# Queries and keys kept as two float16 halves, all score passes on 128 rows, recurrence mixes stored tile by tile

## The chip, the cores and the metric

The kernel runs on one core of one Trainium2 chip. The metric is the time in microseconds (us) that the device takes for one execution. Matrix products run on TensorE (PE; its weight loads are shown as PEld), elementwise work and reductions on VectorE (DVE), activations and casts on ScalarE (ACT), further elementwise work on GpSimd (POOL). SyncE (SP) issues nearly all DMA transfers, one behind another.

## What is computed

One layer of a trunk with two groups of heads that read the same normalised input, 128 context tokens and 1024 latent tokens (T = 1152 columns), model width 1024. Cut to what bears on the change:

```python
p = h @ w_in                                     # h: modulated rms norm of x
q, k, v, g_att, x_lru, g_lru = jnp.split(p, SPLITS, axis=-1)
q, k = axial_rope(q), axial_rope(k)              # latent tokens only
k_all = concatenate([ctx_k, k], axis=1)          # 128 cached keys, of the latent queries' own cache
s = einsum('bqhmd,bkhmd->bhmqk', qblk, k_all) / sqrt(64)   # 8 heads, 2 maps m of 64 wide keys each
p = softmax(s); a = p[:, :, 0] - lam * p[:, :, 1]
o = einsum('bhqk,bkhe->bqhe', a, v_all)
att = rms_norm(o, g_subln) * (1 - lam_init) * silu(g_att)
lru = (hf + hb) * silu(g_lru)                    # scans in both directions over gated inputs
x_new = x + gate * rms_norm(concatenate([att, lru]) @ w_out, g_post)
```

The outputs are the new tokens, the keys and values of the context tokens, and the final states of the scans.

## The kernel before

Every engine works through its instructions in the order in which the program writes them, and so does SP with its DMAs: the order is written out by hand, and a wait holds all that stands behind it on its engine. Tiles come from pools with a fixed number of buffers per tag, and a new tile waits for the last reader of the buffer that it takes.

Float32 matrix operands are kept as a rounded part and a remainder (hi and lo), and a product is three passes, hi by hi, hi by lo and lo by hi (`mm3`, L117 to L119). The projection is computed in blocks of 128 outputs, each of three chunks of 384 columns, each chunk 24 matmuls (`chunk`).

The first stretch of the program works through the eight blocks of the recurrence: two projections and two gates per block on PE, the scans on DVE. `mix_send` writes each block's result to scratch in DRAM, in groups of four blocks (`mixg`). Then come the queries, keys and values (`qk_block`, `v_block`). In a block of queries or keys, `qk_chunk` copies each chunk out of PSUM on ACT; `tick()` after each chunk runs closures that `after(d, fn)` put d ticks later. When the three chunks are there, `rope` rotates the latent columns on DVE (L770 to L773), one tick later `halves` splits the block into hi (a cast on ACT, L745) and lo (a subtraction on POOL, or on DVE for the first block), and one tick after that `send` stores them to the scratch `qs[h]` or `ks`. In the scratch a query tile holds three things for each of 128 queries: the hi part of either map, each written twice (rows 0 to 63 and 64 to 127), and one slot with the lo part of both. For each map the scratch of the keys holds hi in one half of the rows, lo in the other. The cached keys of all heads are loaded, split and stored once (`cached_keys`). Between the blocks stand sums for the gate vector of the output (L930), which wait for a DMA. The first q blocks share the engines with the end of the recurrence's last block (L581 is the square root of its coefficients).

The second stretch is attention, 72 periods of 8 heads by 9 query tiles of 128. Per period PE computes two score maps (`scores`), the product with the values four periods back (`pv`, float16 halves of 128 columns), and pieces of the projection by w_out (`po`). One score map is six passes over 384 keys at most:

```python
PE.matmul(sps[:, j, :w_], lhsT=qt[:, mp], rhs=kt_[:, mp, c], ...)          # L1076: q hi twice x [k hi; k lo]
PE.matmul(sps[:, j, :w_], lhsT=qt[rows, 2], rhs=kt_[rows, mp, c], ...)     # L1078: q lo x k hi, 64 rows
```

DVE takes the maximum out of PSUM (L1085), for the first map adds a small constant (L1088), and ACT computes the exponential out of the same PSUM tile with the row sum (L1092); two such PSUM tiles exist. `recip` and `combine` then form the factor of the second map (L1100, L1102), the difference of the maps (L1111), and its two float16 halves (ACT L1114, POOL L1115), which a DMA transposes for `pv`. Last come the remaining parts of the projection and the output's norm.

Of the kernel before, what the change touches and what calls it, by code (L numbers as in the profile page):

```python
# [10 lines left out]
F32 = mybir.dt.float32  # L11
# [12 lines left out]
NH = 8  # L24
# [74 lines left out]
def hybrid_step_kernel(ctx: ExitStack, tc: tile.TileContext, io):  # L99
# [21 lines left out]
    qs = [dr.tile([P, 3, T], F32R, name=f"qs{h}") for h in range(NH)]  # L121
    ks = dr.tile([P, 2, NH, T + CTX], F32R, name="ks")
    vs = [dr.tile([P, 2, 2, 10, P], F16, name=f"vs{i}") for i in range(NH // 2)]
    sgs = [dr.tile([P, T], F32, name=f"sgs{h}") for h in range(NH)]
    mixg = [dr.tile([P, len(g), 2, T], F32R, name=f"mix{i}") for i, g in enumerate(GROUPS)]
    mix = {kt: mixg[i][:, j] for i, g in enumerate(GROUPS) for j, kt in enumerate(g)}
# [19 lines left out]
    lsig = const.tile([P, 1], F32, name="lsig")  # L146
    gsub = const.tile([P, 1], F32, name="gsub")
# [55 lines left out]
    def load_k(h, mp):  # L203
        if mp == 0:
            kts[h] = kp.tile([P, 2, T + CTX], F32R, tag="kt", name=f"kt{h}")
        move(out=kts[h][:, mp], in_=ks[:, mp, h])
# [5 lines left out]
    def load_q(n):  # L212
        h, i = tiles[n]
        qts[h, i] = kp.tile([P, 3, P], F32R, tag="qt", name=f"qt{h}_{i}", bufs=5)
        move(out=qts[h, i], in_=qs[h][:, :, i * P:(i + 1) * P])

    with ExitStack() as pa:
# [409 lines left out]
        def mix_send(n):  # L627
            for i, m in enumerate(blk.pop(n)["mix"]):
                move(out=mix[KT + n][:, i], in_=m)
# [5 lines left out]
        def next_chunk(n, j):  # L635
# [7 lines left out]
            else:  # L643
                if j == 0:
                    blk["q0"] = lp.tile([P, T], F32, tag="u", name="qfq0")
# [96 lines left out]
        def split_store(t_, w_, name, tags=("a", "w")):  # L742
            hi = lp.tile([P, T], F32R, tag=tags[0], name=f"hi{name}")
            lo = lp.tile([P, T], F32R, tag=tags[1], name=f"lo{name}")
            S.copy(out=hi[:, :w_], in_=t_)  # L745
            split_lo(V if name in ('q0',) else G, lo[:, :w_], t_, hi[:, :w_])
            return hi[:, :w_], lo[:, :w_]

        def cached_keys():
            ck = lp.tile([P, NH * P], F32, tag="xp", name="ck")  # L750
            nc.sync.dma_start(out=ck, in_=io["cache_kT"].rearrange("p h c -> p (h c)"))
            cks = []
            after(2, lambda: cks.extend(split_store(ck, NH * P, "ck")))

            def send():
                for mp in range(2):
                    for part in range(2):
                        r = 64 * (mp ^ part)
# [797 lines left out]
```

## Time and profile before

| | |
|---|---|
| median of 3 runs | 1295.27 us (1294.48 to 1301.24) |
| profiled execution: own time, span | 1297.48 us, 1295.1 us |
| PE, PEld busy | 1220.8 us (94% of the span), 1069.4 us (83%) |
| DVE busy | 968.3 us (75%) |
| ACT, POOL busy | 680.1 us (53%), 479.1 us (37%) |
| mean granted clock of PE | 0.978 of full speed |

The span reaches from the first to the last instruction of the profiled execution; its own time, 2.4 us longer, is what the device counted for the same execution. Busy shares are means over stages with different limits. Matmuls are pipelined, so the duration that the profile gives for one covers a part of the next; what a row of matmuls takes is read from one start to another.

### The profile page before, as it was taken

To read this page: it belongs to the slowest core of one execution; us is meant where nothing else is said; L and a number is where in the kernel's file an instruction comes from. 1 tells how busy PE (TensorE), PEld (TensorE's weight loads), DVE (VectorE), ACT (ScalarE), POOL (GpSimd) and SP (SyncE) were. 2 spreads that over 40 slices of the span, in tenths; PEclk is the share of its full clock that TensorE was granted. 3 is DMA by queue.
4 is the path that set the end of the run, shared out by engine and by line. 5 is a ranking of instruction groups with operands and counts; after the bars stand their busy time and mean duration, and the time that the engine had idled before them with its cause. 6 is when DMAs were issued, how large, how long until landed. Compare 5 with 4: busy or idle time off the path is not lost.

```text
span 1295.1 us, 19733 instructions
## 1 busy us (share of the span) xinstructions
PE 1220.8 (94%) x7672; PEld 1069.4 (83%) x7672; DVE 968.3 (75%) x1253; ACT 680.1 (53%) x1152; POOL 479.1 (37%) x244
## 2 busy tenths in 40 slices
PE   6899999999999899999999699999999989999887
PEld 1499999999999899989999577776777766777666
DVE  4938779777979828666473257888898989899977
ACT  4446545654665233332232357677667676766632
POOL 0421112111212334424242214346655566555624
PEclk9999999999999899999999899999999998999999
DMA  9221222123212757446272659899899988899864
GB/s 364 103 72 41 91 93 93 60 74 111 76 54 102 214 165 220 151 161 167 88 218 68 228 127 201 193 214 249 174 214 224 226 218 191 201 207 217 205 202 167
DMA packets 262916, 208.62 MB, mean 161 GB/s; under 512 B 158876, under 2 KB 228252, under 8 KB 262056
## 3 DMA queue, kind: packets, MB, share of 16 engines
q1 hardware_dynamic: 262536, 206.52, 59.0%
q8 instruction: 60, 0.98, 0.3%
q10 hardware_dynamic: 288, 0.85, 0.2%
q14 instruction: 32, 0.26, 0.1%
HBM read 112.16 MB, written 56.90 MB: 131 GB/s over the span
## 4 chain that ended last, share of the span: by engine, by line
PE 67%; DVE 20%; issue 4%; DMA 4%; ACT 3%; SPq 1%; POOL 1%; DVEq 0%; ACTq 0%; POOLq 0%
PE s L1078 5%; DVE mx L1085 4%; PE s L1076 4%; PE po L117 3%; DVE e L1111 3%; PE ga L119 3%; PE ga L117 3%; PE ga L118 3%; PE po L119 3%; PE po L118 3%; PE v L118 2%; PE v L117 2%; PE v L119 2%; PE x L118 2%; PE x L119 2%
## 5 line engine op out<-in xcount | busy, mean ns | idle before, releaser
L114 POOL TENSOR_TENSOR wlo<-wraw,whi 128x1024 fp32r<-128x1024 f32 x48 | 129.5, 2698 | 421.6 <-ACT whi L262 418.0
L1115 POOL TENSOR_TENSOR a<-e,a 128x1152 f16<-128x1152 f32 (+1 forms) x72 | 156.0, 2166 | 212.3 <-ACT a L1114 210.3
L1085 DVE TENSOR_REDUCE mx<-s 128x1 f32<-128x1152 f32 (+1 forms) x144 | 176.8, 1233 | 65.8 <-PE s L1078 64.1
L1092 ACT ACTIVATE e<-s,mx 128x1152 f32<-128x1152 f32 (+1 forms) x144 | 162.4, 1128 | 77.0 <-DVE fa L1100 29.7
L1111 DVE SCALAR_TENSOR_TENSOR e<-e,fa,e 128x1152 f32<-128x1152 f32 (+1 forms) x72 | 119.0, 1653 | 6.7 <-DVE fa L1102 0.5
L1076 PE MATMUL s<-kt,qt 128*128 128x384 f32 (+1 forms) x400 | 100.3, 355 | 19.5 <-ACT e L1092 18.0
L117 PE MATMUL po<-woh,lt 128*128 128x512 f32 x216 | 97.2, 450 | 16.3 <-ACT e L1092 13.9
L1114 ACT CAST a<-e 128x1152 f16<-128x1152 f32 (+1 forms) x72 | 76.0, 1055 | 60.8 <-DVE e L1111 52.7
L1078 PE MATMUL s<-kt,qt 64*128 64x384 f32 (+1 forms) x400 | 107.0, 369 | 0.0
L117 PE MATMUL pv<-vt,t 128*128 128x128 f16 x584 | 103.5, 222 | 1.9 <-ACT ot L1130 1.9
L118 PE MATMUL pv<-vt,t 128*128 128x128 f16 x584 | 102.8, 220 | 0.0
L119 PE MATMUL pv<-vt,t 128*128 128x128 f16 x584 | 102.8, 220 | 0.0
L1076 PEld LDWEIGHTS s<-kt,qt 128*128 128x128 f32 x400 | 69.1, 192 | 31.8 <-ACT e L1092 24.3
L1078 PEld LDWEIGHTS s<-kt,qt 64*128 64x128 f32 x400 | 63.7, 187 | 34.8 <-issue 34.2
L119 PE MATMUL po<-woh,lt 128*128 128x512 f32 x216 | 86.7, 401 | 0.0
L118 PE MATMUL po<-wol,lt 128*128 128x512 f32 x216 | 86.6, 401 | 0.0
L117 PE MATMUL v<-whi,hTh 128*128 128x256 f32 x288 | 81.8, 284 | 0.0
L119 PE MATMUL v<-whi,hTl 128*128 128x256 f32 x288 | 81.5, 283 | 0.0
L118 PE MATMUL v<-wlo,hTh 128*128 128x256 f32 x288 | 81.5, 283 | 0.0
L117 PEld LDWEIGHTS po<-woh,lt 128*128 128x128 f32 x216 | 41.4, 192 | 41.1 <-issue 15.9
L117 PEld LDWEIGHTS <-t 128*128 128x128 f16 x584 | 57.5, 98 | 17.7 <-issue 17.5
L117 PE MATMUL k<-hTh,whi 128*128 128x384 f32 x192 | 66.4, 346 | 4.8 <-ACT qfk L633 4.8
(299 smaller groups left out, 3588.0 us busy)
## 6 DMA issues: line engine op xcount, KB each, us to landing
wraw<-in_w_in_dram SPq DMA_DIRECT2D x48, 512.0 KB, 3.5
qt<-qs SPq DMA_DIRECT2D x72, 192.0 KB, 3.6
lt<-mix SPq DMA_DIRECT2D x27, 512.0 KB, 4.6
kt<-ks SPq DMA_DIRECT2D x16, 640.0 KB, 6.2
qs<-hiq SPq DMA_DIRECT2D x32, 288.0 KB, 5.8
wa<-in_w_ada_dram SPq DMA_DIRECT2D x16, 512.0 KB, 10.9
wor<-in_w_out_dram SPq DMA_DIRECT2D x32, 256.0 KB, 3.3
mix<-amo SPq DMA_DIRECT2D x6, 1152.0 KB
```

Source lines behind the costliest of these rows:

```text
L114: eng.tensor_tensor(out=lo, in0=val, in1=f(hi), op=ALU.subtract)
L117: PE.matmul(out, lhsT=lh, rhs=rh, start=start, stop=False)
L118: PE.matmul(out, lhsT=lh, rhs=rl, start=False, stop=False)
L119: PE.matmul(out, lhsT=ll, rhs=rh, start=False, stop=stop)
L1076: PE.matmul(sps[:, j, :w_], lhsT=qt[:, mp], rhs=kt_[:, mp, c], start=True, stop=False)
L1078: PE.matmul(sps[:, j, :w_], lhsT=qt[rows, 2], rhs=kt_[rows, mp, c], start=False, stop=True)
L1085: V.tensor_reduce(out=d["mx"][:, mp:mp + 1], in_=sv, axis=AX.XY, op=ALU.max, negate=True)
L1092: S.activation(out=e_[:, :nk].rearrange("p (j c) -> p j c", c=w_), in_=sv, func=AF.Exp, bias=d["mx"][:, mp:mp + 1], accum_out=total)
L1111: V.scalar_tensor_tensor(out=e1, in0=e1, scalar=d["fa"], in1=e0, op0=ALU.mult, op1=ALU.subtract)
L1114: S.copy(out=a16[:, 0:nk], in_=e1)
L1115: G.tensor_tensor(out=a16[:, nk:2 * nk], in0=e1, in1=a16[:, 0:nk], op=ALU.subtract)
```

## The change

Queries and keys are now kept as float16 halves. Each head's q and k block gets a unit, a power of two: ACT squares the block and sums along the rows (`squares`), PE sums that over the partitions with a matrix of ones (`un`, one column), and four small operations on DVE make the power of two from the bits of the sum (`power`; for keys two more keep the factor `back` that undoes both units). ACT scales into the hi half, DVE forms the lo half in one operation. Loading, storing and reading follow that:

- q has four slots per tile: hi and lo of either map, each written twice. The scratch lies tile by tile, so that a tile is one piece of 1 KB per row; the store is eight DMAs in pieces of 256 bytes. A q tile shrinks from 192 to 128 KB, the keys of a head from 640 to 320 KB.
- The cached keys of a head are loaded into the block's own tile, behind its 1152 columns, and handled with it; `cached_keys` is gone.
- Both sets of score passes take 128 rows. The maximum of each map is multiplied by `back` (one more small operation for the second map), the exponential takes it as its scale. The factor of the second map is made by a tensor_scalar.
- The recurrence's mixes of the first two groups are stored tile by tile, in pieces of 512 bytes, and read back in pieces of 4 KB. The mixes of the attention get two buffers of one tag; the gate vector lies in two tiles.

```diff
+            def squares():
+                d["sq"] = lp.tile([P, 1], F32, tag="qsq", name=f"sq{name}")
+                junk = lp.tile([P, T + CTX], F32, tag="gs0" if early else "a", name=f"j{name}")
+                S.activation(out=junk[:, :w_], in_=t_[:, :w_], func=AF.Square, accum_out=d["sq"])
...
-            def halves(tags=("a", "w")):
-                d["hl"] = split_store(t_, T, name, tags)
+            def power():
+                tp = small(f"un{name}")
+                PE.matmul(tp[:, 0:1], lhsT=onesf, rhs=d["sq"], start=True, stop=True)
+                V.tensor_scalar(out=unit, in0=tp[:, 0:1], scalar1=2.0 ** -60, scalar2=None, op0=ALU.max)
+                ui = unit.bitcast(I32)
+                V.tensor_scalar(out=ui, in0=ui, scalar1=0x7FFFFFFF, scalar2=1, op0=ALU.bitwise_and,
+                                op1=ALU.logical_shift_right)
+                V.tensor_scalar(out=ui, in0=ui, scalar1=-1, scalar2=0x663759DF, op0=ALU.mult, op1=ALU.add)
+                V.tensor_scalar(out=ui, in0=ui, scalar1=0x7F800000, scalar2=None, op0=ALU.bitwise_and)
+                if which:
+                    V.tensor_tensor(out=back[:, h:h + 1], in0=unit, in1=qksc[:, 0, h:h + 1], op=ALU.mult)
+                    V.reciprocal(out=back[:, h:h + 1], in_=back[:, h:h + 1])
+
+            def halves():
+                power()
+                d["hl"] = lp.tile([P, 2, T + CTX], F16, tag="gs2" if early else "w", name=f"hl{name}")
+                hi, lo = (d["hl"][:, x, :w_] for x in range(2))
+                S.activation(out=hi, in_=t_[:, :w_], func=AF.Copy, scale=unit)
+                V.scalar_tensor_tensor(out=lo, in0=t_[:, :w_], scalar=unit, in1=hi, op0=ALU.mult, op1=ALU.subtract)
...
+                        if which:
                             r = 64 * (mp ^ part)
-                            move(out=ks[r:r + 64, mp, h, 0:T], in_=val[64 * mp:64 * mp + 64])
+                            nc.sync.dma_start(out=ks[r:r + 64, h, mp], in_=half)
+                        else:
+                            for r in (slice(0, 64), slice(64, 128)):
+                                nc.sync.dma_start(out=qs[h][r, :, 2 * part + mp],
+                                                  in_=half[:, :T].rearrange("p (t c) -> p t c", t=NT))
...
+            squares()
             if which:
                 after(1, context_keys)
+            rope(t_, name)
+            after(1, halves)
+            after(2, send)
...
-                PE.matmul(sps[:, j, :w_], lhsT=qt[rows, 2], rhs=kt_[rows, mp, c], start=False, stop=True)
+                PE.matmul(sps[:, j, :w_], lhsT=qt[:, 2 + mp], rhs=kt_[:, mp, c], start=False, stop=True)
...
             if mp == 0:
-                V.tensor_scalar(out=d["mx"][:, 0:1], in0=d["mx"][:, 0:1], scalar1=lsig, scalar2=None, op0=ALU.add)
+                V.tensor_scalar(out=d["mx"][:, 0:1], in0=d["mx"][:, 0:1], scalar1=unit, scalar2=lsig, op0=ALU.mult,
+                                op1=ALU.add)
+            else:
+                V.tensor_scalar(out=d["mx"][:, 1:2], in0=d["mx"][:, 1:2], scalar1=unit, scalar2=None, op0=ALU.mult)
...
-            V.scalar_tensor_tensor(out=d["fa"], in0=d["fa"], scalar=lam, in1=kqs[h][:, i:i + 1], op0=ALU.mult,
-                                   op1=ALU.mult)
+            V.tensor_scalar(out=d["fa"], in0=d["fa"], scalar1=lam, scalar2=kqs[h][:, i:i + 1], op0=ALU.mult, op1=ALU.mult)
```

The order of instructions shows three places. The first is ACT where the recurrence ends and the queries begin: `w7_1` is the root of the last coefficients, `q1_1` and `q1_2` are the second and third chunk of head 1's queries, `k0_0` the first of head 0's keys, `hiq0` the hi part of head 0's queries, `whi13` a weight's. Before:

```order
L581 ACTIVATE w7_1_3197<-w7_1_3197 128x1158 [waits DVE_49]
L633 ACTIVATE qfq1_3163<-q1_1_3207 128x384 [waits PE_49]
L745 CAST hiq0_3242<-qfq0_3022 128x1152 [waits DVE_49]
L633 ACTIVATE qfq1_3163<-q1_2_3246 128x384 [waits PE_49]
L262 CAST whi13_3315<-wraw26_3052 128x1024 [waits DMAHW5_49,Pool_49]
L633 ACTIVATE qfk0_3289<-k0_0_3290 128x384 [waits DVE_49,PE_49]
```

Of the change (`jq0` and `jq1` are the squares, `hlq0` the hi half):

```order
L585 ACTIVATE w7_1_3199<-w7_1_3199 128x1158 [waits DVE_49]
L768 ACTIVATE jq0_3205,sqq0_3204<-qfq0_3024 128x1152
L637 ACTIVATE qfq1_3165<-q1_1_3212 128x384 [waits PE_49]
L794 ACTIVATE hlq0_3253<-qfq0_3024,qksc_102 128x1152 [waits DVE_49]
L637 ACTIVATE qfq1_3165<-q1_2_3256 128x384 [waits PE_49]
L768 ACTIVATE jq1_3298,sqq1_3297<-qfq1_3165 128x1152 [waits Activation_49]
L266 CAST whi13_3332<-wraw26_3054 128x1024 [waits DMAHW5_49,Pool_49]
L637 ACTIVATE qfk0_3305<-k0_0_3307 128x384 [waits DVE_49,PE_49]
```

Two passes over a whole block, the squares of q0 and of q1, now stand between the copies out of PSUM; the hi half waits for DVE's unit.

The second place is PE just behind the first chunk of head 0's keys, in the change:

```order
L118 MATMUL k0_0_3307<-hTl7_138,whi12_3050 128x384
L119 MATMUL k0_0_3307<-hTh7_130,wlo12_3051 128x384
L779 MATMUL unq1_3341<-sqq1_3297,onesf_91 128x1 [waits Activation_49]
L117 MATMUL k0_1_3350<-hTh0_123,whi12_3050 128x384
L118 MATMUL k0_1_3350<-hTl0_131,whi12_3050 128x384
```

Before, the matmuls of `k0_1` followed those of `k0_0`; now the one-column matmul `unq1` stands between, and waits for ACT's squares. There is one such matmul in each of the 16 blocks of queries and keys; `unq0` stands behind chunk `q1_1`.

The third is DVE in a period of the attention, query tile 40 and 41 (`s` is a score map in PSUM, `mx` its negated maximum, `kq` the sum of the first map, `sm` that of the second). Before:

```order
L1085 TENSOR_REDUCE mx41_9354<-s41_0_9356 128x1 [waits PE_49]
L1088 TENSOR_SCALAR mx41_9354<-mx41_9354,lsig_101 128x1 [waits DVE_49]
L1100 RECIPROCAL fa40_9404<-sm40_9282 128x1 [waits Activation_49]
L1102 SCALAR_TENSOR_TENSOR fa40_9404<-fa40_9404,lam_100,kq4_8973 128x1 [waits DVE_49]
L1111 SCALAR_TENSOR_TENSOR e40_1_9327<-e40_1_9327,fa40_9404,e40_0_9293 128x1152 [waits DVE_49,Pool_49]
L1085 TENSOR_REDUCE mx41_9354<-s41_1_9413 128x1 [waits PE_49]
L1085 TENSOR_REDUCE mx42_9434<-s42_0_9436 128x1 [waits PE_49]
```

Of the change:

```order
L1093 TENSOR_REDUCE mx41_9563<-s41_0_9565 128x1 [waits PE_49]
L1096 TENSOR_SCALAR mx41_9563<-mx41_9563,back_103,lsig_101 128x1 [waits DVE_49]
L1111 RECIPROCAL fa40_9613<-sm40_9490 128x1 [waits Activation_49]
L1113 TENSOR_SCALAR fa40_9613<-fa40_9613,lam_100,kq4_9177 128x1 [waits DVE_49]
L1121 SCALAR_TENSOR_TENSOR e40_1_9536<-e40_1_9536,fa40_9613,e40_0_9501 128x1152 [waits DVE_49,Pool_49]
L1093 TENSOR_REDUCE mx41_9563<-s41_1_9622 128x1 [waits PE_49]
L1099 TENSOR_SCALAR mx41_9563<-mx41_9563,back_103 128x1 [waits DVE_49]
L1093 TENSOR_REDUCE mx42_9644<-s42_0_9646 128x1 [waits PE_49]
```

One operation of 128x1 comes in behind the second map's maximum, and the factor is made by another kind of operation; the order is otherwise that of before.

## Rows read from the trace of the kernel before

**Rows 1.** Windows view, three stages: busy per engine, clock, DMA share, GB/s.

```profile
106.00:395.00 289.00, 286.86 (x1650) 286.54 (x1648) 240.60 (x207) 165.18 (x187) 50.63 (x20) 1.00 0.23 79
480.00:720.00 240.00, 237.71 (x1557) 234.98 (x1556) 144.23 (x203) 75.49 (x143) 81.68 (x29) 0.99 0.49 147
840.00:1224.00 384.00, 362.39 (x2589) 276.56 (x2587) 342.33 (x458) 265.12 (x519) 225.46 (x122) 0.98 0.93 212
```

**Rows 2.** The page's chain that ended last, shares of the span by line.

```profile
PE s L1078 5%; DVE mx L1085 4%; PE s L1076 4%; PE po L117 3%; DVE e L1111 3%; PE ga L119 3%; PE ga L117 3%; PE ga L118 3%; PE po L119 3%; PE po L118 3%; PE v L118 2%; PE v L117 2%; PE v L119 2%; PE x L118 2%; PE x L119 2%
```

**Rows 3.** Groups of instructions by line, the attention stage.

```profile
L1078 PE MATMUL s<-kt,qt 64*128 64x384 f32 (+1 forms) x400 | 107.0, 369 | 0.0
...
L1076 PE MATMUL s<-kt,qt 128*128 128x384 f32 (+1 forms) x400 | 100.3, 355 | 19.5 <-ACT e L1092 18.0 <-DMA qt<-qs 1.1
...
L1111 DVE SCALAR_TENSOR_TENSOR e<-e,fa,e 128x1152 f32<-128x1152 f32 (+1 forms) x72 | 119.0, 1653 | 6.7 <-DVE fa L1102 0.5
...
L1102 DVE SCALAR_TENSOR_TENSOR fa<-fa,lam,kq 128x1 f32<-128x1 f32 x72 | 45.2, 628 | 2.1
...
L1088 DVE TENSOR_SCALAR mx<-mx,lsig 128x1 f32<-128x1 f32 x72 | 15.3, 212 | 2.1
```

**Rows 4.** Timeline of PE and its weight loads: value passes, one score call.

```profile
803.07 0.23 PE L117 MATMUL pv<-vt,t 128*128 128x128 f16 x1
...
804.53 0.22 PE L119 MATMUL pv<-vt,t 128*128 128x128 f16 x1
...
996.16 0.77 PE L1076 MATMUL s<-kt,qt 128*128 128x384 f32 x3
...
996.86 0.47 PEld L1078 LDWEIGHTS s<-kt,qt 64*128 64x128 f32 x3 [0.25 <-issue]
...
997.58 0.50 PE L117 MATMUL po<-woh,lt 128*128 128x512 f32 x1
```

**Rows 5.** Waits from 754 to 1224 us, DVE: total us, times, longest.

```profile
DVE mx L1085 <- PE s L1078: 45.0, 46, 2.9
```

**Rows 6.** Timeline of DVE and POOL around one lambda factor.

```profile
938.36 1.26 POOL L1040 TENSOR_TENSOR acc<-acc,ev 128x512 f32<-128x512 f32 x1
...
938.73 0.91 DVE L1102 SCALAR_TENSOR_TENSOR fa<-fa,lam,kq 128x1 f32<-128x1 f32 x1
...
939.74 1.42 DVE L1111 SCALAR_TENSOR_TENSOR e<-e,fa,e 128x1152 f32<-128x1152 f32 x1
```

**Rows 7.** Timeline of ACT, DVE and PE from the recurrence into the queries.

```profile
409.24 2.24 ACT L581 ACTIVATE w<-w 128x1158 f32<-128x1158 f32 x2
...
411.16 0.33 PE L117 MATMUL k<-hTh,whi 128*128 128x384 f32 x1
...
414.24 1.16 ACT L745 CAST hiq<-qfq 128x1152 fp32r<-128x1152 f32 x1 [2.39 <-DVE qfq L773]
...
415.30 0.48 ACT L633 ACTIVATE qfq<-q 128x384 f32<-128x384 f32 x1
...
425.61 1.35 DVE L114 TENSOR_TENSOR loq<-qfq,hiq 128x1152 fp32r<-128x1152 f32 x1
...
437.06 0.69 PE L117 MATMUL k<-hTh,whi 128*128 128x384 f32 x1 [4.82 <-ACT qfk L633]
```

**Rows 8.** Timeline of SP, DVE and ACT around the first gate-row sum.

```profile
583.17 3.33 SPq L110 DMA_DIRECT2D qs<-hiq  x4
...
592.83 0.68 DVE L930 TENSOR_TENSOR gb<-gacc,gb 2x512 f32<-2x512 f32 x1 [9.22 <-DMA gb<-in_b_gate_dram]
...
594.22 1.29 DVE L770 STREAM_SHUFFLE rsk<-qfk 128x1024 f32<-128x1024 f32 x1
...
597.94 1.23 DVE L773 TENSOR_TENSOR qfk<-qfk,rsk 128x1024 f32<-128x1024 f32 x1
...
605.33 0.43 ACT L836 COPY vf<-v 128x128 f32<-128x128 f32 x2 [2.38 <-PE v L119]
```

**Rows 9.** Groups of instructions by line: TensorE's one-column float32 matmul.

```profile
L417 PE MATMUL ssq<-onesf,qsum 128*128 128x1 f32 x18 | 2.2, 251 | 0.0
```

More of the change, by code (lines that the diff above doesn't have):

```diff
@@ L644, in next_chunk @@
                 if j == 0:
[L645 removed]
+                    blk["q0"] = lp.tile([P, T + CTX], F32, tag="u", name="qfq0")
                 qk_chunk(0, 0, blk["q0"], j)
@@ L740, in hybrid_step_kernel @@
         swap = [(i + 16) % 32 for i in range(32)]
[L742 to L758, printed above, removed]
-                        move(out=ks[r:r + 64, mp, :, T:],
-                             in_=cks[part][64 * mp:64 * mp + 64].rearrange("p (h c) -> p h c", h=NH))
-            after(2 + 1, send)
-        after(9, cached_keys)
         after(24, weight)
         def rope(t_, name):
-            lat = t_[:, CTX:]
+            lat = t_[:, CTX:T]
             rs = lp.tile([P, LAT], F32, tag="xp", name=f"rs{name}")
@@ L776, in qk_block @@
             name = f"{'qk'[which]}{h}"
-            if (which, h) == (0, 0):
-                t_ = blk["q0"]
-                after(1, lambda: rope(t_, name))
-                after(2, lambda: halves(("gs0", "gs2")))
-                after(3, lambda: send())
-            else:
-                t_ = lp.tile([P, T], F32, tag="u", name=f"qf{name}")
-                for j in range(NCH):
-                    qk_chunk(which, h, t_, j)
-                    tick()
-                rope(t_, name)
-                after(1, lambda: halves(("gs0", "gs2") if (which, h) == (0, 1) else ("a", "w")))
-                after(2, lambda: send())
+            w_ = T + CTX if which else T
+            first, early = (which, h) == (0, 0), (which, h) < (0, 2)
+            t_ = blk["q0"] if first else lp.tile([P, T + CTX], F32, tag="u", name=f"qf{name}")
+            unit = qksc[:, which, h:h + 1]
+            d = {}
+            def squares():
+                d["sq"] = lp.tile([P, 1], F32, tag="qsq", name=f"sq{name}")
+                junk = lp.tile([P, T + CTX], F32, tag="gs0" if early else "a", name=f"j{name}")
+                S.activation(out=junk[:, :w_], in_=t_[:, :w_], func=AF.Square, accum_out=d["sq"])
             def context_keys():
@@ L809, in send @@
+            def halves():
[4 more added lines that the diff above has]
+                V.scalar_tensor_tensor(out=lo, in0=t_[:, :w_], scalar=unit, in1=hi, op0=ALU.mult, op1=ALU.subtract)
+            def send():
+                for part in range(2):
                     for mp in range(2):
-                        for part, val in enumerate((hi, lo)):
+                        half = d["hl"][64 * mp:64 * mp + 64, part]
+                        if which:
@@ L815, in qk_block @@
+            if which:
+                nc.sync.dma_start(out=t_[:, T:], in_=io["cache_kT"][:, h])
+            if first:
+                after(1, lambda: (squares(), rope(t_, name)))
+                after(2, halves)
+                after(3, send)
+                return
+            for j in range(NCH):
+                qk_chunk(which, h, t_, j)
+                tick()
+            squares()
             if which:
                 after(1, context_keys)
+            rope(t_, name)
+            after(1, halves)
```

54 lines of the change are left out of this document (24 added, 30 removed).

## The prediction

> **What bounds the kernel now.** I read the stretches first, then the chain that ended last, then line groups and waits of attention, and last the timeline where the change adds waits. In the stretches [rows 1] the reader is to see that PE is busy nearly all the time in each, that DVE has much room among the queries and keys (144.2 of 240 us) and little in attention (342.3 of 384), and that the granted clock there is 0.98, all but full. The chain [rows 2] gives 5% and 4% of the span to the two sets of score passes, 117 us, and another 7% to DVE's maximum and its difference of the maps: attention is bound by PE with DVE close behind. Its DVE waits 45.0 us in all for score passes, in 46 waits [rows 5]; that is all that it could give if PE were no limit.
>
> **Score passes.** A call of six full passes takes 1.42 us from its first start to the next product's start (996.16 to 997.58), 0.237 per pass [rows 4]. The same 384 columns take 289/1650 = 0.175 us in the recurrence's projections, where all passes have 128 rows [rows 1]. So the excess lies with the 64-row set: its weight loads begin only at 996.86, after 0.25 us of idle time in the loading queue, one for each change between 128 and 64 rows. What float16 does is seen at the values: 26 steps of 128 columns from 803.07 to 804.53 are 0.056 each, 0.168 for 384 [rows 4]. A call becomes 6 x 0.168 = 1.01, at the other bound 6 x 0.175 = 1.05; I take 0.41 off. Two maps of 64 latent tiles make 128 full calls, 128 x 0.41 = 53 us of PE. Of 128 x 1.42 = 182 us the chain held 117, 64%, so **-34**. Bounds: if it counts only where DVE stood waiting, 46 x 0.41 = -19; at most -45 [rows 5]. The Trainium skill ("TensorE: Matmul & The Clock Gate", Part 3: packing small matmuls) says that a weight load overlaps a running matmul only when it addresses other rows of the array, which speaks against 128-row passes. The trace disagrees: full-row passes, each with a load of its own, keep the pace above [rows 1, 4]. By the page's rule nothing would be gained here.
>
> **Small operations.** The unit of the second map's maximum is one more tensor_scalar per period; that of before takes 212 ns [rows 3], so 72 x 0.212 = 15.3 us. It stands ahead of the exponential that frees the PSUM tile. I take half, **+8** (0 if DVE's waits swallow it, +15 if none do). The factor's operation averages 628 ns, three times that, 45.2 us in all [rows 3]; in one instance it runs 938.73 to 939.64 and ends with POOL's operation of 938.36 + 1.26 = 939.62 [rows 6]. A tensor_scalar is nearer to 0.212, and 45.2 - 15.3 = 30 us come free. But if it is the third operand that has DVE wait for POOL, the difference of the maps behind it has one too; its mean of 1653 ns against 1.42 alone [rows 3, 6] shows that it already waits. So only **-5** (0 to -30). The wait would be late in the next operation instead.
>
> **The units' matmuls.** 16 columns of ones at 0.25 us [rows 9]: **+4**, without their waits.
>
> **First place: the recurrence into the queries.** ACT ends the roots at 411.48 [rows 7]. The squares of q0 (1.16, as the hi cast of the same tile) end at 412.6. PE's `unq0` stands behind chunk q1_1; the next chunk q1_2 took 24 x 0.173 = 4.2 and ended at 411.16, so PE is at `unq0` at 407.0 and waits 5.6. Then q1_2 and k0_0 run to 421.0, and PE meets `unq1`. That needs the squares of q1, which on ACT stand behind a copy (0.48) and the hi half of q0, which waits for DVE's unit; DVE comes to that place at 425.61, where the lo part of q0 is now. 425.61 + 4 x 0.212 + 1.16 + 0.48 + 1.16 = 429.3, so PE waits 8.3. What goes is the wait of 4.82 at 437.06, whose cause (ACT behind the same place) is overtaken. 5.6 + 8.3 - 4.8 = **+9** (+5 if the copies come early, +14 if the old wait stays).
>
> **Second place: the gate vector.** DVE's sum waits 9.22 us for its DMA, to 592.83 [rows 8]. That DMA stands on SP behind a q store whose issues take 3.33/4 = 0.83. There are three more, +2.5, and they start later by power and hi, 0.85 + 1.16 = 2.0. The sum moves to 597.3; behind it on DVE stands the rope of the next keys. From 597.3: 1.39 to the rope, 4.95 for it, 6 x 0.212 for the unit, 1.16 for hi, two copies of 0.48 and 1.16 for squares give 608.2, where ACT copies out the values for which PE had come at 605.33 [rows 8]. That is 2.9, and 1 to 3 more for the units' matmul behind the same DVE queue: **+6** (0 if the DMA's own landing decides, +14 if the whole 4.5 counts at the sums behind too).
>
> **What I cost at nothing.** In the blocks of queries and keys DVE gets the unit (0.85 to 1.27), the lo half (1.42, as the difference of the maps) and the wait for hi (1.16), 3.4 to 3.9 us. A block is 72 x 0.175 = 12.6 us of PE; DVE now uses 144.2/240 of it, 7.6, and 11.0 to 11.5 stay under. The cover ends when DVE needs 1.1 to 1.6 us more per block. POOL is relieved of its subtraction (its share is 81.7 of 240). ACT trades a cast for a scaling and adds squares (1.16 per block) at 75.5 of 240 [rows 1]. The smaller loads of q and keys and the longer pieces of the mixes give nothing that PE waits for: score passes wait 1.1 us in all for q [rows 3]. The tail's tiles and gate rows change only buffers: nothing. If DMA room matters, it is where the share is 0.93, in attention [rows 1], and there it falls.
>
> **Sum.** -34 + 8 - 5 + 4 + 9 + 6 = **-12** on the profiled execution's own 1297.5 us (2.4 over its span), so 1285.5. That execution is 2.2 above the median of 1295.27; against the runs this is 1283 to 1284, and I say **1284**.
>
> **Rivals.** Half a per cent, 6.5 us, is about what a measurement here can tell from no change.
> 1. *The gain runs deeper*: all 45 us of DVE's waits go, the small operation hides, the gate place costs nothing: -45 + 0 - 5 + 4 + 5 = -41, 1254. For it: PE is on 64% of the calls. Against: DVE is busy 89% of attention and gets more. 0.13.
> 2. *PE's clock falls*: more idle time on PE would bring stretches at the lower of its two levels (1.2 and 2.4 GHz). After the 4.82 us of idle time the chunk at 437.06 runs its first matmul 0.69 long against 0.33 at 411.16 [rows 7]. If attention's mean went from 0.98 to 0.94, 384 x 0.04 = +16: 1299. Against: PE's work there shrinks by a seventh only. 0.11.
> 3. *The q store's short pieces*: eight DMAs in 256-byte pieces. If an issue costs twice 0.83, a store is 13.3 us against a block of 12.6, +0.7 x 8 = +6: 1289. For it: SP queues everything else behind. Against: the DMA share there is 0.49 [rows 1]. 0.07. The Trainium skill ("DMA: Bandwidth & Descriptors", Specifications) wants at least 512 bytes for full rate, and says that shorter ones are read, modified and written; no row here shows such a store. By that page the sum would be about -6.
> 4. *DVE becomes the bound among the queries and keys*: the other side. Each block's hi half waits for PE, then DVE, and lo and the next rope queue behind it. If DVE overruns its cover by 2 us in 14 blocks, beyond the two places counted, +28: 1311. It decides from 1.1 to 1.6 us of unforeseen DVE time or waiting per block (for instance a lo half of 2.5 instead of 1.42), and costs more than the gain from about 0.9 us of stall in each block. For it: the chain unit, hi, lo crosses three engines in every block. Against: DVE's 40% of room. 0.20.
> 5. *Float16 passes keep the old pace*, a call stays 1.42: -12 + 34 = +22, 1317. Against it stand both paces [rows 1, 4]. 0.06.
>
> **How the numbers follow.** My forecast has 0.43, of which 0.35 lies below 1288.8 (faster) and 0.08 above. Faster: 0.35 + 0.13 = 0.48. Same: 0.08 + 0.11 + 0.07 = 0.26. Slower: 0.20 + 0.06 = 0.26. The forecast's own range is 1270 to 1295, from the bounds of the score passes and the two places. The range of 8 in 10 goes from 1252, which takes in the deeper gain, to 1313, past rival 4; rival 5 and the tails stay out.
>
> **What would show it.** A score call of 1.0 us from start to start, and DVE's wait for scores at some 15 us instead of 45. The factor near 0.22, with the difference of the maps longer than 1653 ns by what POOL held. PE idle ahead of the units' matmuls: 5 and 8 us near 407 and 421, under 0.3 us in the other 14 blocks. The gate sum near 597. A lo half of 1.4 on DVE, q issues near 0.83 on SP. The prediction is wrong if the idle time ahead of the units' matmuls or of the copies adds up to more than 25 us among the queries and keys (rival 4), if the call keeps 1.4 (rival 5), or if DVE hardly waits in attention while the period has not shortened.

## The result, and the profile after

The changed kernel takes 1283.61 us (median of 4 runs, 1283.01 to 1285.2), against 1298.26 before (median of 4, 1294.48 to 1302.82): a ratio of 0.9888, with a 95% interval of 0.9847 to 0.9928. The prediction was 1284, faster. It took 12 us off a median of 1295.27, of three runs; with a fourth the median before is 1298.26, and the measured step is 14.7. The profiled execution took 1283.49 us, its span 1281.7, which is 13.4 shorter than that of the profiled execution before.

The starts of the first matmuls of each stage, from the two traces, say where the difference arose:

| stage, from its first matmul to that of the next (us) | before | after | difference | predicted |
|---|---|---|---|---|
| start to first queries | 379.0 | 377.3 | -1.7 | 0 |
| first queries to first values | 64.9 | 74.3 | +9.4 | +9 |
| first values to first score pass | 287.4 | 297.3 | +9.9 | +4 (units), +6 (gate) |
| first score pass to the tail | 494.5 | 463.2 | -31.3 | -34 + 8 - 5 = -31 |
| tail, to the span's end | 69.3 | 69.6 | +0.3 | 0 |

Every sum agrees with its row within 2 us. The experiments show that some of the terms and causes behind the sums do not.

The windows of the changed kernel, in the stretches of [rows 1]:

```profile
106.00:395.00 289.00, 286.88 (x1648) 286.56 (x1647) 240.36 (x208) 163.43 (x185) 50.52 (x20) 1.00 0.25 79
480.00:720.00 240.00, 233.97 (x1517) 229.42 (x1516) 164.52 (x264) 86.19 (x159) 48.76 (x18) 0.99 0.47 123
840.00:1224.00 384.00, 337.59 (x2774) 251.93 (x2774) 352.28 (x551) 287.40 (x555) 248.51 (x128) 0.98 0.89 205
```

PE falls from 362 to 338 busy in the last stretch, whose last 12 us are the tail in the changed kernel, and DVE, which is now at 352, is the busier of the two. The chain by line (the page's part 4) says the same beside [rows 2]: the score passes are no longer among the fifteen lines listed (the chain still holds 38.6 us of them, against 114 before), and DVE's maximum and difference of the maps lead.

```profile
DVE mx L1093 5%; DVE e L1121 4%; PE ga L119 3%; PE ga L117 3%; PE ga L118 3%; DMA t<-a 3%; POOL a L1125 3%; PE v L117 3%; PE v L119 3%; PE v L118 3%; PE x L118 2%; PE x L119 2%; PE x L117 2%; PE g L117 2%; PE g L119 2%
```

Groups of the attention stage (754 to 1224 us, each shape by itself), which answer to [rows 3]. Two of the kernel before first, since [rows 3] mixes shapes and has no row of the exponential:

```profile
L1092 ACT ACTIVATE e<-s,mx 128x1152 f32<-128x1152 f32 x128 | 156.5, 1223 | 77.0 <-DVE fa L1100 29.7 <-DVE mx L1088 15.7 <-DVE mx L1085 13.0
L1111 DVE SCALAR_TENSOR_TENSOR e<-e,fa,e 128x1152 f32<-128x1152 f32 x64 | 107.5, 1680 | 6.0 <-DVE fa L1102 0.5
```

The changed kernel:

```profile
L1103 ACT ACTIVATE e<-s,mx,back 128x1152 f32<-128x1152 f32 x128 | 168.2, 1314 | 66.9 <-DVE fa L1111 18.7 <-DVE mx L1096 16.3 <-DVE mx L1099 16.1
L1121 DVE SCALAR_TENSOR_TENSOR e<-e,fa,e 128x1152 f32<-128x1152 f32 x64 | 107.8, 1685 | 5.7
L1113 DVE TENSOR_SCALAR fa<-fa,lam,kq 128x1 f32<-128x1 f32 x72 | 19.5, 271 | 2.1
L1096 DVE TENSOR_SCALAR mx<-mx,back,lsig 128x1 f32<-128x1 f32 x71 | 19.2, 271 | 2.1
L1099 DVE TENSOR_SCALAR mx<-mx,back 128x1 f32<-128x1 f32 x72 | 15.4, 214 | 2.1
```

The factor (L1113) takes 271 ns where it took 628, and the difference of the maps behind it takes on average what it took before, 1685 ns against 1680 (128x1152). The new operation (L1099) takes the 0.21 us that was assumed. The exponential takes 1314 ns, against 1223 for this shape before; the prediction had no term for that.

Waits, 771 to 1212 us, total, times and longest. [rows 5] is of a longer stretch, so the same stretch of the kernel before comes first:

```profile
DVE mx L1085 <- PE s L1078: 41.3, 43, 2.9
PE s L1076 <- ACT e L1092: 18.0, 20, 2.4
```

```profile
PE s L1084 <- ACT e L1103: 40.0, 42, 2.5
DVE mx L1093 <- PE s L1086: 18.3, 24, 2.6
```

DVE waits 18 us for score passes instead of 41 (some 15 were forecast). In turn PE waits 40 us instead of 18 for the exponential to free a PSUM tile.

A score call in PE's timeline, beside [rows 4]:

```profile
999.33 0.66 PE L1084 MATMUL s<-kt,qt 128*128 128x384 f16 x3
999.83 0.65 PE L1086 MATMUL s<-kt,qt 128*128 128x384 f16 x3
1000.32 0.22 PE L117 MATMUL pv<-vt,t 128*128 128x128 f16 x1
```

From 999.33 to 1000.32 a call is 0.99 us, where it was 1.42. Where the recurrence meets the queries, PE and ACT, beside [rows 7]:

```profile
411.95 0.59 PE L779 MATMUL unq<-sqq,onesf 128*128 128x1 f32 x2 [6.47 <-ACT jq L768]
...
412.87 0.52 PE L118 MATMUL q<-hTl,whi 128*128 128x384 f32 x1
413.19 0.52 PE L119 MATMUL q<-hTh,wlo 128*128 128x384 f32 x1
...
424.48 1.25 ACT L794 ACTIVATE hlq<-qfq,qksc 128x1152 f16<-128x1152 f32 x1 [12.20 <-DVE qksc L785]
...
427.45 0.59 PE L779 MATMUL unq<-sqq,onesf 128*128 128x1 f32 x2 [4.73 <-ACT jq L768]
```

Both waits of the forecast are there, 6.47 and 4.73 us (5.6 and 8.3 forecast). Behind each, PE runs at the lower of its two levels (1.2 instead of 2.4 GHz; the granted clock is 0.50 from 412 to 416 and from 428 to 433): the matmuls of 412.87 and 413.19 stand 0.32 apart instead of 0.17.

The sums for the gate vector, DVE, ACT and PE, beside [rows 8]:

```profile
604.59 0.68 DVE L938 TENSOR_TENSOR gb<-gacc,gb 2x512 f32<-2x512 f32 x1 [6.73 <-DMA gb<-in_b_gate_dram]
...
678.71 1.26 ACT L794 ACTIVATE hlq<-qfq,qksc 128x1152 f16<-128x1152 f32 x1 [7.14 <-DVE qksc L785]
679.87 0.47 ACT L637 ACTIVATE qfk<-k 128x384 f32<-128x384 f32 x1
680.24 0.61 ACT L922 CAST ghl<-gwhs 128x512 fp32r<-128x512 f32 x1
...
680.90 0.40 PE L930 MATMUL gacc<-ghl,pick 128*2 128x512 f32 x1 [1.31 <-ACT ghl L922]
...
682.07 0.40 PE L930 MATMUL gacc<-ghl,pick 128*2 128x512 f32 x1 [0.77 <-DVE ghl L114]
```

The first sum comes at 604.59. PE is some 10 us behind by then, from the places ahead, so this is about 2 us late against 592.83, not 4.5. The loss lies elsewhere: ACT's scaling into the hi half waits 7.14 us for DVE's unit, the cast for the second gate sum stands behind it, and PE waits for that cast.

### The profile page after: what moved, and what is told of

Its sections match the earlier page's. It is cut to its first block, busy times and chain, and to the rows that moved or that the text cites. A ratio compares the mean times of both kernels' runs of the same rounds, so it can differ in the third digit from the quotient of the medians.

```text
span 1281.7 us, 19990 instructions
## 1 busy us (share of the span) xinstructions
PE 1174.4 (92%) x7704; PEld 1022.1 (80%) x7704; DVE 990.8 (77%) x1420; ACT 709.2 (55%) x1183; POOL 445.0 (35%) x228
## 4 chain that ended last, share of the span: by engine, by line
PE 51%; DVE 26%; ACT 6%; DMA 6%; POOL 5%; issue 4%; SPq 1%; DVEq 0%; ACTq 0%; POOLq 0%
DVE mx L1093 5%; DVE e L1121 4%; PE ga L119 3%; PE ga L117 3%; PE ga L118 3%; DMA t<-a 3%; POOL a L1125 3%; PE v L117 3%; PE v L119 3%; PE v L118 3%; PE x L118 2%; PE x L119 2%; PE x L117 2%; PE g L117 2%; PE g L119 2%
## 5 line engine op out<-in xcount | busy, mean ns | idle before, releaser
L114 POOL TENSOR_TENSOR wlo<-wraw,whi 128x1024 fp32r<-128x1024 f32 x48 | 126.2, 2630 | 560.7 <-ACT whi L266 560.7
L1103 ACT ACTIVATE e<-s,mx,back 128x1152 f32<-128x1152 f32 (+1 forms) x144 | 175.5, 1219 | 67.9 <-DVE fa L1111 18.7
L1084 PE MATMUL s<-kt,qt 128*128 128x384 f16 (+1 forms) x400 | 88.2, 325 | 41.8 <-ACT e L1103 40.3
L1121 DVE SCALAR_TENSOR_TENSOR e<-e,fa,e 128x1152 f32<-128x1152 f32 (+1 forms) x72 | 113.7, 1579 | 6.4
L117 PE MATMUL po<-woh,lt 128*128 128x512 f32 x216 | 100.1, 463 | 19.2 <-DMA lt<-mix 13.9
L1084 PEld LDWEIGHTS <-qt 128*128 128x128 f16 x400 | 33.5, 97 | 72.1 <-issue 60.7
L1086 PE MATMUL s<-kt,qt 128*128 128x384 f16 (+1 forms) x400 | 87.9, 325 | 0.0
L119 PE MATMUL po<-woh,lt 128*128 128x512 f32 x216 | 87.3, 404 | 0.0
L117 PE MATMUL x<-hTh,whi 128*128 128x384 f32 x192 | 65.4, 341 | 2.1 <-DVE hTh L400 2.1
```

Source lines behind the costliest of these rows:

```text
L114: eng.tensor_tensor(out=lo, in0=val, in1=f(hi), op=ALU.subtract)
L117: PE.matmul(out, lhsT=lh, rhs=rh, start=start, stop=False)
L119: PE.matmul(out, lhsT=ll, rhs=rh, start=False, stop=stop)
L1086: PE.matmul(sps[:, j, :w_], lhsT=qt[:, 2 + mp], rhs=kt_[:, mp, c], start=False, stop=True)
L1103: S.activation(out=e_[:, :nk].rearrange("p (j c) -> p j c", c=w_), in_=sv, func=AF.Exp, bias=d["mx"][:, mp:mp + 1], scale=unit, accum_out= ...
L1121: V.scalar_tensor_tensor(out=e1, in0=e1, scalar=d["fa"], in1=e0, op0=ALU.mult, op1=ALU.subtract)
```

## The experiments

Times are medians; ratios are against runs of the kernel before. The stretch from the first score pass to the tail is read from the profiled execution of each kernel, which lies up to 3 us from the kernel's median (experiment 8: 1268.76 against 1271.81), so a few us between two such stretches are not sure.

**1. Only the 128 rows.** Edit of the kernel before:

```diff
-                PE.matmul(sps[:, j, :w_], lhsT=qt[rows, 2], rhs=kt_[rows, mp, c], start=False, stop=True)
+                PE.matmul(sps[:, j, :w_], lhsT=qt[:, 2], rhs=kt_[:, mp, c], start=False, stop=True)
```

> The kernel before, with one edit: its second set of float32 score passes takes all 128 rows instead of 64. (The products then also hold terms of the other map and of k's remainder, so the scores are not those of the reference; the count and the size of the passes are those of the changed kernel.) My theory, that the excess of a score call is the weight load at each change between 128 and 64 rows, expects a call of 6 x 0.175 = 1.05 us instead of 1.42, an attention stage shorter by 30 to 40 us, with no added small operations, and 1297 - 35 = about 1260 us, between 1254 and 1268. The rival, that float16 is what makes the passes fast, expects a call still at 1.42 and 1295 us, within 4.

Measured: 1283.68 us, ratio 0.9889 (0.9864 to 0.9913). First score pass to the tail: 481.7 instead of 494.5. A call on PE:

```profile
1002.21 0.79 PE L1076 MATMUL s<-kt,qt 128*128 128x384 f32 x3
1002.83 0.68 PE L1078 MATMUL s<-kt,qt 128*128 128x384 f32 x3
1003.35 0.39 PE L117 MATMUL po<-woh,lt 128*128 128x512 f32 x1
```

The second set takes 1002.83 to 1003.35, 0.52, which is 0.17 a pass in float32: there the rows do it, not the type. The whole call takes 1.14, neither the 1.05 expected nor the 1.42 of [rows 4]; the first set keeps 0.62. From 1.14 to the changed kernel's 0.99 is left to float16. The gain is 13 us, far from 35. Of two theories one had the cause of the second set right and the size of the gain wrong.

**2. 64 rows in float16.** Edit of the changed kernel:

```diff
-                PE.matmul(sps[:, j, :w_], lhsT=qt[:, 2 + mp], rhs=kt_[:, mp, c], start=False, stop=True)
+                PE.matmul(sps[:, j, :w_], lhsT=qt[rows, 2 + mp], rhs=kt_[rows, mp, c], start=False, stop=True)
```

> The changed kernel, with its second set of score passes on 64 rows again (float16, q's remainder by k's hi part; the product of the two remainders is left out). The theory of the weight loads expects the cost to come back, but only in part, since a float16 load of 64 or 128 rows takes about 97 ns where a float32 one took 190: a call of about 1.0 + 4 x 0.05 = 1.2 us, and 1288 to 1296 us instead of 1283.6. If the width of the data alone decides, the call stays at 1.0 and the time at 1283.6, within 2.

Measured: 1295.33 us, ratio 0.9979 (0.9964 to 0.9994); first score pass to the tail 474.3 instead of 463.2. PE and its weight loads:

```profile
1030.81 0.65 PE L1085 MATMUL s<-kt,qt 128*128 128x384 f16 x3
1031.39 0.66 PE L1087 MATMUL s<-kt,qt 64*128 64x384 f16 x3
...
1031.39 0.27 PEld L1087 LDWEIGHTS <-qt 64*128 64x128 f16 x3 [0.32 <-issue]
1031.98 0.31 PEld L1176 LDWEIGHTS s<-ident,ot 128*128 128x128 f32 x3 [0.32 <-issue]
```

1.17 us from 1030.81 to 1031.98. The loading queue stands idle for 0.32 at both changes of the row count (0.25 in the call of [rows 4]). Against 0.99 the two changes cost 0.18, or 0.09 each; in float32 they cost 1.42 - 1.14 = 0.28, or 0.14 each. Call and time came as this theory expected, at the long end: the price comes back in part.

**3. The factor in its old form.** Edit of the changed kernel:

```diff
-            V.tensor_scalar(out=d["fa"], in0=d["fa"], scalar1=lam, scalar2=kqs[h][:, i:i + 1], op0=ALU.mult, op1=ALU.mult)
+            V.scalar_tensor_tensor(out=d["fa"], in0=d["fa"], scalar=lam, in1=kqs[h][:, i:i + 1], op0=ALU.mult,
+                                   op1=ALU.mult)
```

> The changed kernel, with the factor of the second map made by a scalar_tensor_tensor again, as before the change. The prediction's step (the wait for POOL is only handed to the next operation, worth 5 us) expects the factor at about 630 ns, the difference of the maps shorter by some of that, and 1287 to 1289 us. Its rival comes from the trace of the change: the factor takes 271 ns there and the difference of the maps did not become longer (1579 against 1653 ns), so the wait belonged to the form of the operation and went away; it expects the 26 us of DVE time back, DVE being the busier engine of attention now, and 1295 to 1305 us.

Measured: 1300.65 us, ratio 1.003 (1.0012 to 1.0048): with this one line the change as a whole is lost. First score pass to the tail: 479.5 instead of 463.2. The factor takes 478 ns on average there, and the difference of the maps became no shorter (1775 ns against 1685). My step is refuted, its rival holds.

**4. The small operation left out.** Edit of the changed kernel, with the undoing factor at one:

```diff
-            else:
-                V.tensor_scalar(out=d["mx"][:, 1:2], in0=d["mx"][:, 1:2], scalar1=unit, scalar2=None, op0=ALU.mult)
...
-                    V.reciprocal(out=back[:, h:h + 1], in_=back[:, h:h + 1])
+                    V.reciprocal(out=back[:, h:h + 1], in_=onesf[:, 0:1])
```

> The changed kernel without the small operation that scales the second map's maximum; the factor that undoes the units is set to one so that all numbers stay finite (the scores then stay in units, and the output is not the reference's). The prediction's step (72 operations of 0.21 us, half of them on the path) expects 8 us less, about 1276 us. If DVE's slack in attention swallows them, 1283 within 2; if each stands on the path, and its hand-over to ACT with it, 15 to 20 us less, 1264 to 1269.

Measured: 1274.66 us, 9.0 less than the change. Between the two profiled executions the stretch from the first score pass to the tail is 7.3 shorter (455.8 against 463.2). The +8 holds.

**5. Hi half one chunk later.** Edit of the changed kernel, all blocks but the first two (`power()` is called by itself, `halves` no longer calls it):

```diff
-            after(1, halves)
-            after(2, send)
+                after(1, power)
+                after(2, halves)
+                after(3, send)
```

> The changed kernel, with the unit's matmul and its small operations where they are, but the scaling into the hi half, the lo half and the store one chunk later, in all blocks of queries and keys but the first two. If the stall at the second sum for the gate vector (PE waits 1.3 and 0.8 us there, and its clock is at the lower level for 3.4 us after) comes from ACT's scaling, which waits 7.1 us for DVE's unit with the copies behind it, those 4 us go: 1279 to 1280 us. If the lateness lies on DVE itself, nothing changes: 1283.6, within 2. If the later stores or the longer hold on the buffers make new waits: 1286 or more.

Measured: 1276.06 us, ratio 0.9837 (0.9795 to 0.9879), 7.5 us less than the change. The first score pass starts at 741.0 instead of 748.9, and PE meets the second gate sum without idle time:

```profile
674.92 0.34 PE L119 MATMUL k<-hTh,wlo 128*128 128x384 f32 x1
675.09 0.63 PE L934 MATMUL gacc<-ghl,pick 128*2 128x512 f32 x2
675.56 0.33 PE L117 MATMUL k<-hTh,whi 128*128 128x384 f32 x1
```

So the loss sat in ACT's queue. The gain is twice what was expected, because the waits at the first gate sum (2.2 and 0.8 us in the change) nearly went as well: PE waits 1.2 us in all for both sums.

**6. The first place reordered.** Edit of the changed kernel, first two blocks only:

```diff
-                after(2, halves)
-                after(3, send)
+                after(3, power)
+                blk['hi0'] = halves
+                after(4, send)
...
             squares()
+            if (which, h) == (0, 1):
+                blk['hi0']()
```

> The changed kernel, with the first two blocks of queries reordered: the unit's matmul of the first block one chunk later, and on ACT the squares of the second ahead of the first's hi half. If the two waits of PE (6.5 and 4.7 us by the trace, each with a stretch at the lower clock behind it) come from these places in the queues, both go; the old wait of 4.8 us comes back, some 2 us longer because the lo half now stands behind the unit and the hi half: the step from the first chunk of queries to the values is 66.5 to 68 us instead of 74.3, and the time 1277 to 1278 us. If DVE's lateness at the end of the recurrence is what counts, the wait only moves to the next place: 1283.6, within 2.

Measured: 1284.11 us, no change; first queries to first values 74.7 instead of 74.3. The wait at the first unit shrinks to 1.15 us, that at the second is gone, and two others of PE stand behind them (the first and the last row):

```profile
430.23 0.45 PE L117 MATMUL k<-hTh,whi 128*128 128x384 f32 x1 [2.42 <-DVE qksc L780]
...
430.78 1.26 ACT L793 ACTIVATE hlq<-qfq,qksc 128x1152 f16<-128x1152 f32 x1 [14.18 <-DVE qksc L785]
...
443.34 0.58 PE L779 MATMUL unk<-sqk,onesf 128*128 128x1 f32 x2 [6.95 <-ACT jk L768]
```

So this reordering gains nothing, as the rival expected. That DVE's lateness at the recurrence's end is the cause fits (its unit for the first block lets ACT scale at 424.48 above, and the copies, the hi and the lo half all follow it), but it is argued, not shown: the edit also put that unit later on DVE, so that ACT scales at 430.78 here, and no run made DVE earlier.

**7. The factor alone, in the kernel before** (the line of experiment 3, the other way round):

> The kernel before, with only the factor of the second map made by a tensor_scalar. After the runs so far I expect the three-operand form to be what waits for POOL: the factor at 0.27 us instead of 0.63, 26 us of DVE time free. As DVE waits 45 us for score passes in that kernel, a part only counts: 6 to 14 us less, 1283 to 1291. The prediction's step expects 5 us, about 1292; if the wait moves to the next operation, 1297.5, within 2.

Measured: 1286.81 us, ratio 0.9911 (0.9878 to 0.9945); first score pass to the tail 481.9, 12.6 less. POOL and DVE there:

```profile
935.89 1.28 POOL L1040 TENSOR_TENSOR acc<-acc,ev 128x512 f32<-128x512 f32 x1
936.23 0.27 DVE L1102 TENSOR_SCALAR fa<-fa,lam,kq 128x1 f32<-128x1 f32 x1
936.61 1.78 DVE L1110 SCALAR_TENSOR_TENSOR e<-e,fa,e 128x1152 f32<-128x1152 f32 x1
```

The factor runs while POOL works; the difference of the maps, begun at 936.61, takes 1.78 instead of 1.42: POOL's operation has 0.56 left and ends at 937.17. In [rows 6] the old form ended with POOL's operation. So an operation of DVE on two tensors waits for what is left of POOL's operation at its own start. All 64 differences of this shape fit that within 0.02 us: 1.42, or 1.22 and what is left where that is more; so do the 64 of the changed kernel, and of the 72 old factors all but one (0.22, or what is left); in that one, as in two of the 64 differences before, POOL's operation began up to 0.03 us behind DVE's and held it as well. The operation behind pays for the rest of POOL's operation only if there is a rest, as here: over the stage its mean does not grow (1658 ns for this shape, 1680 before).

**8. Rows and factor together, in the kernel before** (experiments 1 and 7):

> The kernel before, with its second set of float32 score passes on 128 rows and the factor by a tensor_scalar, and nothing else of the change. If the two gains help each other (PE frees DVE's waits, DVE takes the time), attention is as short as in the changed kernel without its added small operation, 456 to 466 us from the first score pass to the tail, and nothing is lost among the queries and keys: 1263 to 1271 us, below the changed kernel. If the gains are the same time counted twice, no better than the better of them alone: 1280 to 1284.

Measured: 1271.81 us, ratio 0.9791 (0.9757 to 0.9826); 465.7 from the first score pass to the tail, 28.7 less than before, where the two alone give 12.8 + 12.6 = 25.4 (the 3.3 between them is about what the profiled execution here lies under its median). Two edits of one statement each beat the changed kernel by 12 us: the attention is nearly as short, and nothing is lost among the queries and keys (first score pass at 731.0). As in experiment 1, the scores hold a product too many, that of the other map's q remainder and this map's k remainder.

**9. The mixes tile by tile** (the change's edits to the stores and loads of the mixes, on experiment 8):

> The kernel before with three parts of the change: 128 rows, the tensor_scalar factor, and the recurrence's mixes of the first two groups stored tile by tile. The prediction costs the mixes at nothing: 1271.8 us, within 2, as without them. In that kernel the mean share of the DMA engines in attention is 1.00 and PE and DVE wait some 6 us for loads of keys and queries; if the shorter pieces of the old layout are what fills the DMA engines, the share falls and 3 to 6 us go: 1266 to 1269.

Measured: 1273.7 us against 1271.8, DMA share 0.99 against 1.00 (771 to 1212 us): nothing, as costed.

**10. Weights of w_out earlier** (on experiment 8; the first eight loads ahead of keys, queries and values, the split of the first four within the last projection block):

```diff
+        for kt in GROUPS[0]:
+            load_wo(kt, 0)
         for n in range(2):
             load_k(0, n)
...
+        after(2, first_half)
         for h in range(len(AMONG) + 1, NH):
             g_block(gp_, h)
```

Only the first four loads are in fact ahead of keys, queries and values; the second four follow behind them.

> The kernel before with 128 rows and the tensor_scalar factor, and, outside the change, the first eight pieces of w_out loaded ahead of the first keys, queries and values, the first four of them split during the last projection block. If the 14 us for which PE stands at the start of attention, before and after the change, come from these loads (the last waits in the queue to about 740 us), 4 to 7 us go: 1265 to 1268 us. If something else holds the start, 1271.8, within 2.

Measured: 1268.25 us, ratio 0.9778 (0.9753 to 0.9804), the lowest median here. In experiment 8 (first row) PE stands 14.86 us; here 7.69, and still waits for loads of the mixes:

```profile
746.18 0.77 PE L117 MATMUL po<-woh,lt 128*128 128x512 f32 x1 [14.86 <-DMA lt<-mix]
```

```profile
741.58 0.76 PE L117 MATMUL po<-woh,lt 128*128 128x512 f32 x1 [7.69 <-DMA lt<-mix]
```

Its median lies 3.6 us below that of experiment 8, but the intervals of the two ratios overlap: that it is the faster of the two is likely, not shown.

**11. The exponential without its scale operand** (edit of the changed kernel, `scale=unit` left out, the factor at one as in experiment 4):

> The changed kernel, with the exponential's scale operand left out and the factor that undoes the units set to one (the scores stay in units, so the output is not the reference's). In the trace of the change an exponential takes 1314 ns where it took 1223 before; the prediction had no term for that. If the scale operand, a tile with one number per row, is the cause, the exponential is back at 1.22 us, 144 x 0.09 = 13 us of ACT; PE waits 40 us for exponentials in the changed kernel, so half of it or more should count: 5 to 10 us less, 1274 to 1279. If something else makes it longer (the two engines' reads of PSUM at once, for instance), it stays at 1.31 and the time at 1283.6.

Measured: 1280.46 us (1276.51 to 1283.03), 3 less than the change, and its exponential:

```profile
L1103 ACT ACTIVATE e<-s,mx 128x1152 f32<-128x1152 f32 x128 | 156.5, 1223 | 71.1 <-DVE fa L1111 20.7 <-DVE mx L1099 18.7 <-DVE mx L1096 16.9
```

The operand costs 91 ns each, as thought; but first score pass to the tail is 462.2, only 1.0 less. It is hidden nearly whole, and the 5 to 10 us do not come.

**12. Loads as large as before** (edit of the changed kernel):

```diff
-        qts[h, i] = kp.tile([P, 4, P], F16, tag="qt", name=f"qt{h}_{i}", bufs=5)
-        nc.sync.dma_start(out=qts[h, i], in_=qs[h][:, i])
+        first = min(4 * i, 4 * NT - 7)
+        tile_ = kp.tile([P, 7, P], F16, tag="qt", name=f"qt{h}_{i}", bufs=5)
+        qts[h, i] = tile_[:, 4 * i - first:4 * i - first + 4]
+        nc.sync.dma_start(out=tile_, in_=qs[h].rearrange("p t s c -> p (t s) c")[:, first:first + 7])
```

> The changed kernel, with each load of a query tile made 224 KB instead of 128 (it takes in slots of a neighbouring tile that nothing reads), so that queries and keys of a head come to 2336 KB of loads instead of 1472; before the change they were 2368. The prediction costs the smaller loads at nothing: 1283.6 us, within 2, whatever the DMA share. The rival comes from a sum over the runs so far: the kernel before with 128 rows and the new factor takes 465.7 us from the first score pass to the tail, the changed kernel 463.2 although it has a small operation more that costs 7.3, so float16 and the smaller loads together are worth some 10 us there; the shorter call (0.98 against 1.05) can hold at most 9 of them and more likely half. If the loads hold the other half, by late transposes and queries, it takes 4 to 7 us more, 1288 to 1291, with a DMA share near 1.0 instead of 0.87.

Measured: 1284.93 us against 1283.61, first score pass to the tail 463.6 against 463.2, with the DMA share up to 0.94 from 0.87 (771 to 1212 us): nothing. The rival falls, as far as a share of 0.94 can say: the 1.00 of experiment 8 is not reached.

## Why the prediction was right, point by point

That the time came within a us of 1284 is luck: two terms of attention were wrong by about as much, in opposite directions.

**Score passes, -34.** Mechanism right in the main, size wrong. The call fell as forecast, and of its 0.43 the row count makes 0.28 (experiment 1); the rest comes with float16, where the prediction put nearly all of it down to the 64-row set. In all the passes gave some 23 to 27 us (the stage's 31.3, with the 7.3 and 1.0 of added work put back and the factor's 12.6 to 16.3 taken off). The 128 rows alone give 12.8, 16.1 where the factor is already cheap (481.9 to 465.7), and 11.1 in the changed kernel (experiment 2). The step that failed is "the chain held 117 of 182 us, 64%": that a line stands on the chain does not mean that the time comes free when it shrinks, for PE then waits longer for the exponential (40 us instead of 18).

What float16 adds is not measured by itself: the changed kernel takes 463.2 with a small operation that costs 7.3 and an exponential that costs 1.0, so without them 454.9, 10.8 under experiment 8, uncertain by some 3. Loads (experiment 12) are not it; 128 calls of 0.99 instead of the 1.14 of experiment 1 would be 19 us of PE, an estimate from two calls. That the passes account for it, and not the changed buffers of the mixes, is argued, not shown.

The Trainium skill ("TensorE: Matmul & The Clock Gate", Part 3: packing small matmuls) has, in its list of what overlaps, weight loads overlap only where other rows are addressed; the paragraph on the mechanism also lets a load into a background buffer go ahead. The runs do not bear out the list: passes of 128 rows, each with a load of its own, follow each other every 0.17 us, and the queue stands idle for 0.25 to 0.32 us where the row count changes.

**Small operation, +8.** Right: 7.3 (experiment 4).

**Factor, -5.** The step that failed is "So only -5", since the next operation would take over the wait. The wait is not handed on as a whole: 12.6 us alone, 16.3 within the change (experiments 7 and 3), while the mean of the differences stays (1658 and 1685 ns against 1680). It lies between the bounds of 0 and 30. The surplus of the score passes' term and the deficit of this one cancelled, which is why the stage's sum was right. The Trainium skill ("VectorE: DVE Perf Modes", two Vector instructions with no wait between them) counts the second tensor input of an operation with two in SBUF among what is read through an interface shared with GpSimd. The trace agrees: with two tensors the factor ended with POOL's operation [rows 6], with scalars per row it ran during one (936.23, in 0.27 us).

**Units' matmuls, +4.** Smaller, and not measured by itself: with experiment 5 the stage from the first values to the first score pass is 1.6 us longer than before, and 13 of the 16 units, forecast at 0.25 each, stand in it.

**First place, +9.** Measured +9.4, in the places named: the waits of 6.47 and 4.73 came and the old one of 4.82 went, 6.4 together. The second wait was shorter than forecast, and the lower clock, not counted, made up for it: behind the two waits 27 matmuls of 384 columns stand 0.32 apart or more instead of 0.17, behind the old wait 17, some 1.6 us; the two units' matmuls at that clock take 0.45 each. Whether the places in the queues or DVE's lateness behind them is the cause stays open (experiment 6).

**Second place, +6.** Size near, place wrong: of the stage's +9.9, 8.3 go with experiment 5. The DMA of the first sum came hardly later. The loss is in ACT's queue, where the scaling into hi waits for DVE and holds the cast that PE needs.

**At nothing.** The mixes and the loads: confirmed (9 and 12). DVE's added work in the blocks stays hidden: 164.5 of 240 us. The exponential's scale was missed, and is worth 1 to 3.

**Rivals.** None came. The 256-byte stores were issued at 5.93 us for eight (0.74 each, less than before). The mean granted clock of the stretches of [rows 1] stayed within 0.01; it fell in the stretch of the first place (395 to 480 us: 0.92 instead of 0.96).

## What to carry to other kernels

Count the changes of the row count between matmuls as well as the passes: each cost 0.14 us here in float32 and 0.09 in float16. A line's share of the chain bounds what it can give, and the next engine's slack says what it will; when two engines are close, undo each part alone before believing a sum that fits. Where an engine's queue takes an operation that waits for another engine's late result, put it behind the copies that a third engine needs: one chunk later was worth 7.5 us here.

## What was not expected of the hardware

An operation of DVE on one number per row cost, by its form, as much as the row count of all score passes (12.6 and 12.8 us, each alone): 628 ns on average with two tensor operands, 271 with scalars per row. The form is not slow in itself: where POOL was not at work as it began, the old one took 0.22 us (20 of its 72), less than the new. An exponential with a scale per row takes 1314 ns where one without takes 1223, and the price is the same with 128 columns instead of 1152: 458 against 366.
